# Loading the 32-blocks of a batch for the triangular substitution: four DMAs of 32 rows in place of one DMA with four copies as its outermost dimension

## The chip, the cores and the metric

The kernel runs on one core of one Trainium2 chip. The metric is the device time of one execution in microseconds (us), the median over several runs. The core has five engines that work side by side, each in the order of its own instruction queue: TensorE (PE, matmuls), VectorE (DVE), ScalarE (ACT), GpSimd (POOL) and SyncE (SP). SP only issues DMAs here; ACT and POOL issue some as well. The transfers themselves run on 16 DMA engines.

## The reference, cut to what matters

The reference is two network blocks over 512 tokens of width 1024. The part that the change touches is the bidirectional state recurrence of the second block, computed over 256 context tokens and then over the 512 latent tokens, in both directions:

```python
def wkv_step(S, inp):
    r, w, k, v, a, b = inp
    sa = jnp.einsum('dbhvk,dbhk->dbhv', S, a)
    S = S * w[..., None, :] + sa[..., None] * b[..., None, :] + v[..., None] * k[..., None, :]
    return S, jnp.einsum('dbhvk,dbhk->dbhv', S, r)

def wkv_bidir(S0, r, k_mod, v, decay, a_vec, b_vec):
    ...
    xs = tuple(to_scan(u) for u in (both(r), decay, k_mod, both(v), both(a_vec), b_vec))
    S, ys = lax.scan(wkv_step, S0, xs)
    ...
```

## The kernel before, in words

The recurrence is not run token by token. It is cut into chunks of 64 tokens, 12 chunks for each direction (4 of context, 8 latent). Two chunks make a batch, so there are 12 batches, taken in turn from the two directions. Within a chunk the recurrence becomes a matrix form that needs the inverse of a triangular 64x64 matrix for each of 8 heads. That inverse is found from the inverses of its two 32x32 diagonal blocks. A batch holds 2 chunks x 8 heads x 2 diagonal blocks = 32 such blocks.

Each batch passes through four steps, each a Python function:

- `ph_a` (L1130 on) loads what the chunk needs (`kb`, `kr`), scales it (`cs`, `ep`, `em`, `AR`, `BK`) and builds the products `AMB` with matmuls (`pA`, `ptb`).
- `ph_i` writes the 32 diagonal blocks from `AMB` to `atD` in DRAM by four DMAs of 32 KB (L1183), and loads them back as `LT` (L1186). In `LT` a partition holds one whole 32x32 block (1024 numbers, 4 KB), and the 32 blocks stand four times below each other, so that the 128 partitions hold four copies.
- `ph_s` runs the substitution on VectorE: 31 steps of two operations, a product into `Tm` from `LT` and `Ti` (L1198), and an addition into `Ti` (L1200). The four copies each work on another quarter of the columns, which `Ti` gets from a constant (L1193). Then four DMAs write `Ti` to `ttD` (L1203).
- `ph_b` loads the inverses into `TT` by four DMAs (L1217) and `v` into `XV` or `XW` (L1212, L1213), then works with matmuls (`pi`, `px`, `pW`, `pch`) and copies between PSUM and SBUF until the batch's state and output are there.

`LT` has two buffers, as `Ti` has; `Tm` has one. `batch(n)` calls `ph_a` and `ph_i` of batch n, then `ph_s` of the batch before, and `ph_b` of the batch two before.

The program is written step by step, but a planner settles the order in each engine's queue when the program is built. It walks through the instructions with estimates of their durations and waits, and it keeps an engine fed with whatever is ready: around the recurrence stand the projections of the second block (matmuls `pf`, `pt`, with weights loaded into `wr` at L298 and split by L305 on ACT and L306 on VectorE), the gates (`mth`, L1354) and the preparation of queries and keys (`dq`, `dk`, `gk`, `boD`). On the chip the order is then fixed; an instruction whose input is late holds up everything behind it on its queue.

All the loads named here go out from SP's queue, in order.

Of the kernel before, what the change touches and what calls it, by code (L numbers as in the profile page):

```python
# [191 lines left out]
def _build(ctx, tc, A, out, dbg, upto):  # L192
    nc = tc.nc
    V, SC, GP, PE, SY = nc.vector, nc.scalar, nc.gpsimd, nc.tensor, nc.sync
# [59 lines left out]
    def t2(name, dt=F32, w=512, tag="t2"):  # L254
        return cur["bp"].tile([128, w], dt, tag=tag, name=name, bufs=NB[tag])
# [7 lines left out]
    def ps(name, tag="mm"):  # L263
        return cur["pp"].tile([128, PB[tag][1]], F32, tag=tag, name=name, bufs=PB[tag][0])
# [21 lines left out]
    def vv(name):  # L286
        o, w = _VOFF[name]
        return vec[:, o:o + w]
# [182 lines left out]
    for i in range(4):  # L471
        t = t2("x%d" % i, w=1024, tag="t4")
# [569 lines left out]
    for f in range(8):  # L1042
        src, g = (ya[f], vv("norm_rec")[:, f:f + 1]) if f < 4 else (yb[f - 4], vv("norm_att")[:, f - 4:f - 3])
# [56 lines left out]
    atD = [dp.tile([2, 2, 8, 32, 32], F32, name="atD%d" % i) for i in range(4)]  # L1100
# [6 lines left out]
    def w1(name, shape=(4, 64), bufs=1, dt=F32):  # L1107
        p = rp if name == "AZ" else rpa if name in EARLY else rpb
        return p.tile([128] + list(shape), dt, tag=name, name=name, bufs=bufs)
# [10 lines left out]
    for d in range(2):  # L1120
        for e in range(2):
            t = rp.tile([128, 4, 64], F32, name="SI%d%d" % (d, e))
# [55 lines left out]
    def ph_i(d, AMB, bi):  # L1178

        for e in range(2):  # L1180
            for i in range(2):
                r0 = 64 * e + 32 * i
                SY.dma_start(atD[bi][e, i].rearrange("q s t -> s q t"),  # L1183
                             AMB[r0:r0 + 32, e, :, :, 32 * i:32 * i + 32].rearrange("p s f t -> p (s f) t"))
        LT = w1("LT", (32, 32), 2)
        SY.dma_start(LT.rearrange("p s t -> p (s t)"),  # L1186
                     atD[bi].rearrange("e i q s t -> (e i q) (s t)")[None].to_broadcast([4, 32, 1024]))
        return LT

    def ph_s(d, LT, bi):  # L1190
# [144 lines left out]
    def batch(n):  # L1335
        d, chs = batches[n]
        AMB = w1("AMB", (2, 2, 4, 192), 3)
        sts = {c - min(chs): ph_a(d, c, c - min(chs), AMB) for c in chs}
        LT = ph_i(d, AMB, n % 4)
        while loops:  # L1340
            ph_s(*loops.pop(0))
        loops.append((d, LT, n % 4))
        pend.append((n, (d, chs, sts, AMB, n % 4)))
        if len(pend) > 2:
            run_b()
# [61 lines left out]
    for j, nm in enumerate(("q", "k")):  # L1407
        g = qkg[:, 64 * j:64 * j + 64]
# [35 lines left out]
    for nm, c0, db in (("q", 512, "ql"), ("k", 1024, "kl")):  # L1444
        for hf in range(2):
# [30 lines left out]
            for f in range(2):  # L1476
                p = ps("dqT", "mm")
# [294 lines left out]
    def ot(name, bufs, w=512):  # L1772
        return orp.tile([128, w], F32, tag=name, name=name, bufs=bufs)
# [6 lines left out]
    for i in range(4):  # L1780
        t = op_.tile([128, 1024], F32, name="acc%d" % i)
# [13 lines left out]
    for c in range(4):  # L1795
        po2 = [ps("po2", "aux" if c % 2 else "mm") for _ in range(2)]
        for kh in range(2):
            hi, lo = split_chunk(load_chunk(A["w_out_2"], 256 * c, kt=4, nw=256, k0=4 * kh))
            for i in range(4):
                sl = slice(128 * i, 128 * (i + 1))  # L1800
                p = po2[i // 2][:, 256 * (i % 2):256 * (i % 2) + 256]
# [7 lines left out]
        for i in range(4):  # L1809
            t = ot("x2t", 3, 256)  # L1810
# [5 lines left out]
        for f in (2 * c, 2 * c + 1):  # L1816
            p = ps("xT", "aux")
            for i in range(4):
                PE.transpose(p[:, 128 * i:128 * (i + 1)], acc[i][:, 128 * f:128 * (f + 1)], ident)
            t = ot("xT", 2)  # L1820
# [217 lines left out]
    for i in (3, 2, 1, 0):  # L2038
# [5 lines left out]
        else:  # L2044
            t = t2("xn", w=1024, tag="t4")
# [33 lines left out]
    for p in range(16):  # L2079
        g, pr = p // 2, p % 2  # L2080
# [57 lines left out]
```

## Time and profile before

| what | value |
|---|---|
| median of 3 runs | 1914.18 us (1913.24 to 1919.19) |
| the profiled execution | 1915.38 us, of which the span from first to last instruction is 1913.6 us |
| TensorE | busy 1723.1 us, 90% of the span |
| VectorE | busy 1067.9 us, 56% |
| ScalarE | busy 616.6 us, 32% |
| GpSimd | busy 227.2 us, 12% |
| the batches of the recurrence | from about 495 us to about 1130 us of the span |
| the `LT` loads | 12, of 512 KB, the first issued at 502.7 us, the last at 1041.1 us |

The shares are means over the whole span, in which the projections come first, the recurrence with more projections next, and the experts at the end; each stage has another limit. A wait that the profile names ("<-DMA LT<-atD") is the event that came last before the waiting instruction started. The chain of work that ended last is followed back from the last instruction, at each step to what released it, so that its pieces add up to the span.

### The profile page before, as it was taken

How to read it: one execution, taken by the hardware profiler on the slowest of the kernel's cores; microseconds unless marked ns; L12 is line 12 of the kernel's file. 1: busy time of each engine (PE TensorE's matmuls, PEld its weight loads, DVE VectorE, ACT ScalarE, POOL GpSimd, SP SyncE). 2: the span in 40 equal slices, each digit the busy share in tenths (PEclk: the TensorE clock that was granted, in tenths of full speed). 3: DMA queues.
4: the chain of work that ended last, by engine and by line, in shares of the span. 5: the costliest groups of instructions: out<-in, count | busy, mean ns of one | idle time of the engine just before them, and what ended most of it. 6: DMA issues, size and time to landing. Idle time of an engine off the chain costs nothing.

```text
span 1913.6 us, 31328 instructions
## 1 busy us (share of the span) xinstructions
PE 1723.1 (90%) x12309; PEld 1225.2 (64%) x12310; DVE 1067.9 (56%) x2489; ACT 616.6 (32%) x1154; POOL 227.2 (12%) x254
## 2 busy tenths in 40 slices
PE   6999998976789798988989979979889999999998
PEld 3974678863456676877778756868854445444444
DVE  3545676565478655977877736866432323332332
ACT  4334464453443232333423424452311111111110
POOL 0200002011113001122110013300100000000000
PEclk8999999988898897989989988999989999999999
DMA  8336623558547545555664365717359999999997
GB/s 300 120 113 218 213 77 120 201 169 284 153 113 196 141 137 122 146 130 148 165 151 106 113 240 203 246 33 276 137 200 386 387 386 386 386 387 386 386 386 277
DMA packets 277023, 417.33 MB, mean 218 GB/s; under 512 B 105068, under 2 KB 128136, under 8 KB 276616
## 3 DMA queue, kind: packets, MB, share of 16 engines
q1 hardware_dynamic: 247976, 384.88, 60.5%
q10 hardware_dynamic: 25568, 16.78, 2.9%
q0 software_dynamic: 3328, 13.63, 2.5%
q8 instruction: 98, 1.61, 0.4%
q14 instruction: 53, 0.43, 0.1%
HBM read 371.70 MB, written 43.53 MB: 217 GB/s over the span
## 4 chain that ended last, share of the span: by engine, by line
PE 70%; DMA 11%; DVE 10%; ACT 3%; issue 3%; SPq 1%; POOL 1%; ACTq 0%; DVEq 0%; POOLq 0%
PE ped L1982 6%; PE peg L1943 6%; PE peu L1950 6%; PE pf L311 4%; PE pf L313 4%; PE pf L312 4%; PE pcb L2014 3%; PE po L1805 2%; DMA LT<-atD 2%; PE pt L313 2%; PE pt L311 2%; PE pW L1286 2%; PE pg L1916 2%; PE pt L312 2%; PE pg L1917 2%
## 5 line engine op out<-in xcount | busy, mean ns | idle before, releaser
L306 DVE TENSOR_TENSOR wl<-wr,wh 128x1024 fp32r<-128x1024 f32 x125 | 153.4, 1227 | 73.9 <-ACT wh L305 70.4
L305 ACT ACTIVATE wh<-wr 128x1024 fp32r<-128x1024 f32 x125 | 131.9, 1056 | 184.5 <-PE pf L312 91.9
L311 PE MATMUL pf<-h2h,wh 128*128 128x512 f32 x344 | 143.4, 417 | 20.0 <-ACT mth L1354 12.5
L313 PE MATMUL pf<-h2h,wl 128*128 128x512 f32 x344 | 141.4, 411 | 0.0
L312 PE MATMUL pf<-h2l,wh 128*128 128x512 f32 x344 | 141.3, 411 | 0.0
L1943 PE MATMUL peg<-wg,hTg 128*64 128x512 f32 x512 | 127.8, 597 | 0.0
L1982 PE MATMUL ped<-wd,hid 128*64 128x512 f32 (+1 forms) x528 | 125.5, 585 | 0.7 <-ACT hid L1966 0.7
L1950 PE MATMUL peu<-wu,hTg 128*64 128x512 f32 x512 | 126.0, 594 | 0.0
L1198 DVE TENSOR_TENSOR Tm<-LT,Ti 128x60 f32<-128x60 f32 (+24 forms) x372 | 86.6, 233 | 55.8 <-DMA LT<-atD 47.5
L2015 DVE TENSOR_TENSOR acc<-acc,pcb 128x512 f32<-128x512 f32 (+1 forms) x124 | 75.8, 665 | 39.9 <-PE pcb L2014 39.7
L1988 POOL TENSOR_TENSOR yl<-ey,yh 128x512 fp32r<-128x512 f32 x30 | 38.3, 1277 | 467.3 <-ACT yh L1987 467.3
L311 PEld LDWEIGHTS pf<-h2h,wh 128*128 128x128 f32 x344 | 67.1, 195 | 37.9 <-ACT mth L1354 12.8
L1200 DVE TENSOR_TENSOR Ti<-Ti,Tm 128x60 f32<-128x60 f32 (+24 forms) x372 | 83.8, 225 | 8.8
L1950 PEld LDWEIGHTS peu<-wu,hTg 128*64 128x64 f32 x512 | 44.4, 137 | 65.0 <-issue 63.3
L1982 PEld LDWEIGHTS ped<-wd,hid 128*64 128x64 f32 x528 | 38.9, 136 | 70.4 <-issue 64.7
L1943 PEld LDWEIGHTS peg<-wg,hTg 128*64 128x64 f32 x512 | 41.4, 137 | 61.9 <-issue 58.6
L313 PEld LDWEIGHTS pf<-h2h,wl 128*128 128x128 f32 x344 | 66.6, 194 | 21.7 <-issue 5.2
L312 PEld LDWEIGHTS pf<-h2l,wh 128*128 128x128 f32 x344 | 67.1, 195 | 17.4 <-issue 2.6
L1987 ACT ACTIVATE yh<-ey 128x512 fp32r<-128x512 f32 x30 | 18.9, 630 | 165.9 <-DVE ey L1986 94.1
L1923 DVE TENSOR_SCALAR hTg<-pg,gs,sh 128x128 f32<-128x128 f32 x64 | 25.3, 408 | 76.3 <-PE peu L1950 38.4
L1920 ACT ACTIVATE hTg<-pg,sh,gs 128x128 f32<-128x128 f32 x64 | 28.1, 456 | 122.6 <-PE peu L1950 55.4
L311 PE MATMUL pt<-wh,h1h 128*128 128x256 f32 x192 | 56.2, 295 | 5.8 <-ACT q L547 3.7
(958 smaller groups left out, 4327.8 us busy)
## 6 DMA issues: line engine op xcount, KB each, us to landing
wg<-in_w_exp_gate_dram SPq DMA_DIRECT2D x64, 1024.0 KB
wu<-in_w_exp_up_dram SPq DMA_DIRECT2D x64, 1024.0 KB
wd<-in_w_exp_down_dram SPq DMA_DIRECT2D x62, 1024.0 KB
wr<-in_w_in_dram SPq DMA_DIRECT2D x97, 512.0 KB
kb<-kbD SPq DMA_DIRECT2D x24, 384.0 KB
wr<-in_w_out_dram SPq DMA_DIRECT2D x16, 512.0 KB
LT<-atD SPq DMA_DIRECT2D x12, 512.0 KB
thD<-mth ACTq DMA_DIRECT2D x24, 256.0 KB
```

Source lines behind the costliest of these rows:

```text
L305: SC.activation(hi, raw, AF.Copy)
L306: V.tensor_tensor(lo, raw, hi.bitcast(F32), ALU.subtract)
L311: PE.matmul(p, ah, bh, start=start, stop=False)
L312: PE.matmul(p, ah, bl, start=False, stop=False)
L313: PE.matmul(p, al, bh, start=False, stop=stop)
L1198: V.tensor_tensor(tmp[:, :nj, :n], bc(LT[:, s, None, ts_], [128, nj, n]), bc(T[:, js, s:s + 1], [128, nj, n]), ALU.mult)
L1200: V.tensor_tensor(T[:, js, ts_], T[:, js, ts_], tmp[:, :nj, :n], ALU.add)
L1943: mm = PE.matmul(pg[64 * a:64 * a + 64, :], hT[:, k, 64 * a:64 * a + 64], gp[a][k // 4][:, k % 4, :], start=(k == 0), stop=(k == 7), tile_ ...
L1950: PE.matmul(pu[64 * a:64 * a + 64, :], hT[:, k, 64 * a:64 * a + 64], up[a][k // 4][:, k % 4, :], start=(k == 0), stop=(k == 7), tile_posit ...
L1982: PE.matmul(pd[64 * a:64 * a + 64, :], hid[:, m * k + 64 * a:m * k + 64 * a + 64], dn[q][a][:, k, 0:q1 - q0], start=(k == 0), stop=(k == 3 ...
L2014: PE.matmul(p, ohT[R, 128 * i:128 * (i + 1)], yy[R, qs], start=(z == 0), stop=(z == len(parts) - 1))
L2015: V.tensor_tensor(acc[i][:, qs], acc[i][:, qs], p, ALU.add)
```

## The change

`ph_i` loads `LT` by four DMAs, one for each group of 32 partitions, each of which reads the same 32 rows of 4 KB from `atD`. Before, it was one DMA whose source has a leading dimension of four copies with step 0. The bytes that move, their rows and where they land are the same; `atD`, the store before it and the substitution behind it are not touched.

```diff
         LT = w1("LT", (32, 32), 2)
-        SY.dma_start(LT.rearrange("p s t -> p (s t)"),
-                     atD[bi].rearrange("e i q s t -> (e i q) (s t)")[None].to_broadcast([4, 32, 1024]))
+        for g in range(4):
+            SY.dma_start(LT[32 * g:32 * g + 32].rearrange("p s t -> p (s t)"),
+                         atD[bi].rearrange("e i q s t -> (e i q) (s t)"))
         return LT
```

## Rows read from the trace of the kernel before

**Rows 1.** The page: busy time of TensorE, and the chain by engine.

```profile
PE 1723.1 (90%) x12309; PEld 1225.2 (64%) x12310; DVE 1067.9 (56%) x2489; ACT 616.6 (32%) x1154; POOL 227.2 (12%) x254
...
PE 70%; DMA 11%; DVE 10%; ACT 3%; issue 3%; SPq 1%; POOL 1%; ACTq 0%; DVEq 0%; POOLq 0%
```

**Rows 2.** Five of the chain's nine longest pieces in the recurrence: start, us, what.

```profile
502.68 10.43 DMA LT<-atD
550.55 11.31 DMA kb<-kbD
...
746.18 11.13 DMA TT<-ttD
...
917.76 9.58 DMA boD<-gk
955.36 13.02 DMA wr<-in_w_in_dram
```

**Rows 3.** The nine pieces as windows, sum (us, busy by engine); LT's four.

```profile
sum 103.32, PE 84.98 PEld 69.02 DVE 40.26 ACT 26.74 POOL 14.76; mean PE 9.44 PEld 7.67 DVE 4.47 ACT 2.97 POOL 1.64
...
sum 45.32, PE 39.09 PEld 31.98 DVE 13.56 ACT 13.70 POOL 6.21; mean PE 9.77 PEld 8.00 DVE 3.39 ACT 3.43 POOL 1.55
```

**Rows 4.** SP's queue, four of the 12 LT loads: start, us, line, what.

```profile
549.89 0.55 SPq L1186 DMA_DIRECT2D LT<-atD  x1
...
745.05 0.56 SPq L1186 DMA_DIRECT2D LT<-atD  x1
...
913.13 0.56 SPq L1186 DMA_DIRECT2D LT<-atD  x1
...
954.76 0.55 SPq L1186 DMA_DIRECT2D LT<-atD  x1
```

**Rows 5.** The chain's pieces of other DMAs: start, us, what.

```profile
689.91 1.63 DMA atD<-AMB
...
735.92 4.47 DMA kb<-kbD
...
986.68 1.87 DMA TT<-ttD
```

**Rows 6.** Who waited for LT (us, times), and VectorE's first use of two loads.

```profile
  DVE Tm L1198: 47.5, 8
...
513.13 0.19 DVE L1198 TENSOR_TENSOR Tm<-LT,Ti 128x31 f32<-128x31 f32 x1 [12.05 <-DMA LT<-atD]
...
1049.63 0.19 DVE L1198 TENSOR_TENSOR Tm<-LT,Ti 128x31 f32<-128x31 f32 x1 [4.75 <-DMA LT<-atD]
```

**Rows 7.** The load at 1041.07: SP's issue, DMA queue in 1042 to 1045, window.

```profile
1041.07 0.56 SPq L1186 DMA_DIRECT2D LT<-atD  x1
...
q1 hardware_dynamic: 51, 0.21, 21.0%
...
1042.00:1045.00 3.00, 3.00 (x57) 2.73 (x54) 2.70 (x11) 1.18 (x2) 0.00 (x0) 1.00 0.23 75
...
1600.00:1603.00 3.00, 3.00 (x14) 1.52 (x11) 0.17 (x1) 0.60 (x1) 0.00 (x0) 1.00 1.05 386
```

**Rows 8.** Windows by stage: us, engines' busy us (instructions), PEclk, DMA share, GB/s.

```profile
495.00:740.00 245.00, 205.57 (x1411) 154.11 (x1412) 162.54 (x405) 85.57 (x136) 37.33 (x49) 0.86 0.54 145
740.00:930.00 190.00, 168.50 (x1907) 145.48 (x1905) 146.86 (x477) 65.97 (x131) 35.78 (x49) 0.92 0.59 144
930.00:1130.00 200.00, 186.63 (x2092) 159.64 (x2093) 146.12 (x449) 67.61 (x127) 17.94 (x36) 0.95 0.51 141
```

**Rows 9.** Eleven gaps of TensorE behind the loads as windows: first, last, sum.

```profile
508.87:521.33 12.46, 0.00 (x1) 0.01 (x1) 8.09 (x16) 3.13 (x4) 1.42 (x3) 0.61 0.23 70
...
1049.63:1051.67 2.04, 0.00 (x1) 0.00 (x1) 1.94 (x8) 0.59 (x1) 0.00 (x0) 1.00 0.09 15
sum 58.45, PE 0.03 PEld 0.10 DVE 37.23 ACT 14.01 POOL 7.56; mean PE 0.00 PEld 0.01 DVE 3.38 ACT 1.27 POOL 0.69
```

**Rows 10.** SP's queue where four loads took long to issue.

```profile
873.61 10.73 SPq L1429 DMA_DIRECT2D gk<-kbD  x4
```

## The prediction, made before the changed kernel was run

> **What bounds the kernel now.** I read the page first. TensorE is busy for 90% of the span, and the chain of work that ended last gives it 70%, but 11% of the chain is DMA and another 10% VectorE [rows 1]. So the kernel is bound by TensorE on average and by something else in places; the question is whether the `LT` load is one of these places.
>
> Next I asked for the chain's longest pieces. Between 495 and 1130 us, the stage of the recurrence, its nine longest are all DMAs of 9.6 to 13.0 us [rows 2], and their sum is 103.3 us [rows 3]. Four are the `LT` load itself, 45.3 us together [rows 3]. SP's queue shows what the other five are: `kb` at 550.55, `TT` at 746.18, `wr` at 955.36 and `boD` at 917.76 [rows 2] went out 0.7, 1.1, 0.6 and 4.6 us after an `LT` load [rows 4], and so did one more `wr` behind another. On the chain an `atD` store costs 1.63 us, a `TT` load 1.87 and a `kb` load of 384 KB 4.47 when no `LT` load stands ahead [rows 5]. So `LT` costs time twice: VectorE waits for it, 47.5 us in 8 of the 12 batches [rows 6], and what is issued behind it lands late.
>
> Third, why it takes so long. The load at 1041.07 is the one with the least beside it. In 1042 to 1045 its queue moved 51 packets, 0.21 MB, in 21.0% of 16 engines' time, at 75 GB/s; the expert stage moves 386 GB/s [rows 7]. 21.0% of 16 x 3 us is 10.1 engine-us, or 198 ns for one 4 KB packet. The load has 128 such packets: 25.3 engine-us. VectorE got the data 8.56 us after the issue [rows 6, 7]. A load on four engines needs 6.3 us for its packets and leaves 2.2 us for issue, start and completion, which is near the whole of the 1.87 us of a small `TT` load [rows 5]; 16 engines would need 1.6 us. The busy share of about a quarter says the same: four engines work, twelve idle. Four is the size of the source's outermost dimension.
>
> **The change, part by part.** Removed: 12 DMAs of 512 KB. Added: 48 of 128 KB, each with 32 rows as the outermost dimension on both sides. The same 128 packets move. No row shows a 32-row DMA of 4 KB packets, so I bound it: below by the 32-row `atD` store, 1.63 us, above by the `kb` load of 128 rows, 4.47 us [rows 5].
>
> The Trainium skill, "DMA: Bandwidth & Descriptors", section "Rules for kernel authors", says that a leading zero-stride broadcast of c copies confines a DMA to at most c engines, and that a multiple of 16 belongs outermost; 21% of the engines' time in the trace agrees for four [rows 7]. By the Trainium skill, same page, section "Why a DMA increments its semaphore by 16 and not by 1", 32 outermost rows use 16 engines, which no row here shows for such rows.
>
> *The load.* Issuing one costs SP 0.55 us [rows 4]. So the fourth goes out 3 x 0.55 = 1.65 us after the first, and lands 1.6 to 4.5 us later: 3.3 to 6.1 us in all. I take 2.65 us for that landing, 4.3 in all: nearer to the store, which has the same 32 rows, than to the `kb` load, which moves three times the bytes of a part. The four `LT` pieces of the chain, 45.3 us [rows 3], become 17.2: **28.1 us less** (21 to 32 by the bounds).
>
> *What stands behind it.* The five other pieces sum to 103.3 - 45.3 = 58.0 us [rows 3]. Without the long queue I give `kb`, the two `wr` and `boD` 4.5 us each and `TT` 1.9 [rows 5], and each is issued 1.65 us later, because SP now has four DMAs ahead of it: 4 x 6.2 + 3.6 = 28.4, **29.6 us less**. By the chain alone 57.7 us would go.
>
> *What takes its place.* The chain follows one path only, and beside these waits TensorE was working: inside the nine pieces it is busy for 85.0 of 103.3 us, idle for 18.3 [rows 3]. Its queue is in a fixed order, so it gains only where it stood still. It stood still in the whole stage for 635 - 560.7 = 74.3 us [rows 8]. I matched its gaps to the loads: eleven, of 58.5 us together [rows 9], begin within 19 us of the issue of an `LT` load and end on ACT or VectorE work that was itself waiting behind `LT`, or behind a transfer held up by it. The first is plain: VectorE stood 12.05 us for `LT` [rows 6], and TensorE until 521.33 for an emptied PSUM tile [rows 9]. A load that lands earlier can take at most its 57.7 / 9 = 6.4 us from each gap; four gaps are longer than that and give 25.6, the seven shorter ones taken whole 22.9, together 48.5 us. The lower bound is the 18.3 us that TensorE idles inside the nine pieces themselves. I take the middle, **33 us**, because neither end fits: part of each gap lies after the landing, so 18.3 is too little, but VectorE was still busy for 37.2 of the gaps' 58.5 us [rows 9] with substitution steps and work queued behind them, of which some will be late for other reasons.
>
> *Costed at nothing.* SP's 36 more issues are 20 us of its queue over 540 us; they cost something only where SP itself is late, and the 1.65 us above is that price. `atD`, `Tm`, `Ti` and TensorE's own work don't change. TensorE's mean granted clock is 0.86 in 495 to 740 and 0.61 in the first gap [rows 8, 9], so it fell from its 2.4 GHz level to 1.2 there after standing still; fewer gaps may give some back, which I leave to the range.
>
> *The sum.* The profiled execution took 1915.4 us, 1.2 above the median of the runs. 1915.4 - 33 = 1882.4, or **1881 us** beside the median. Its own range is 48.5 to 18.3 us less, 1866 to 1896. The planner's order is a further unknown: it places 36 more instructions, and may order the other queues anew from 495 us on. A misplaced instruction costs about one gap of the kind seen here, up to 12.5 us [rows 9]; I widen both ends by that: 1854 to 1909.
>
> **The rivals.**
>
> *TensorE absorbs it.* TensorE is busy in 82% of the nine pieces [rows 3], and its order is fixed. If the work behind each load is late for another reason anyway (PSUM not emptied, a `wr` not split), only the idle time inside the pieces goes: 18.3 us, 1896 us. For it: 90% TensorE. Against: the gaps behind the pieces wait on engines that had themselves waited for `LT`.
>
> *Nothing changes.* The load stays on few engines, or the time lies in reading back what was just stored, not in the engines. Then 1912 to 1915 us. Against it: 51 packets in 3 us, evenly, is a rate limit and no latency [rows 7].
>
> *Slower: SP's queue becomes the limit.* Four `gk` loads took SP 10.73 us to issue at 873.61 [rows 10], while an `LT` load was under way. So issuing can be held up by what is already queued. If each of the four parts waits like that, at 10.73 / 4 = 2.7 us, the fourth goes out 8.1 us after the first, and `LT` lands at 10.7, no sooner than now. What stands behind goes out at 4 x 2.7 = 10.7 and lands 4.5 later, at 15.2 us, against 0.65 + 58.0 / 5 = 12.2 now: 3.0 x 5 = 15 us more, 1929 us. It decides from 2 us for each issue on, where both land as late as now (8.56 and 12.2). Against it: the `LT` issues themselves took 0.55 us each [rows 4], and the backlog at 873.61 may be the four engines' own, which the change takes away.
> The Trainium skill, "DMA: Bandwidth & Descriptors", section "Rules for kernel authors", also says that two transfers to disjoint partition halves serialize and should be one, which speaks for this rival; no run so far shows two parts of one load.
>
> **How the numbers follow.** Forecast 0.60; TensorE absorbs it 0.22; nothing changes 0.08; slower 0.10. The range 1854 to 1909 holds the first two, 0.82. Within 0.3% (5.7 us, about what a measurement of this kernel can tell from no change) is 1908 to 1920. Faster: the first two and a little of the third, 0.83. Same: 0.08. Slower: 0.09, since a little of the last case lies within 0.3%.
>
> **What the profile would show.** Right: 48 `LT` DMAs; issue to first use of about 4 to 5 us; VectorE's wait for `LT` from 47.5 to about 10 us; no DMA piece above 8 us on the chain between 495 and 1130; TensorE's idle time in the recurrence from 74 to about 41. Wrong: if `LT` lands in under 5 us and TensorE's idle time stays, the gaps had other causes; if L1186 or the instruction behind it shows long issues, the slow rival holds; if the queues' order differs far from the load, the planner's part is larger than the load's.

## The result, and the profile after

The changed kernel takes 1866.94 us (median of 4 runs, 1863.63 to 1868.35), the kernel before beside it 1914.12: a ratio of 0.975, with a 95% interval of 0.9728 to 0.9772. It is 47 us faster, where 33 were forecast; the time lies in the range. The profiled execution took 1868.35 us. Behind L1187 every line number is one higher than before.

The page of the changed kernel, to be read beside [rows 1]; its third line is a group (line, engine, operation, tiles, count | busy us, mean ns | idle time before it and what ended it):

```profile
PE 1715.4 (92%) x12309; PEld 1216.4 (65%) x12310; DVE 1068.7 (57%) x2489; ACT 617.4 (33%) x1154; POOL 230.4 (12%) x254
...
PE 73%; DVE 11%; DMA 7%; ACT 3%; issue 3%; SPq 2%; POOL 1%; ACTq 0%; DVEq 0%; POOLq 0%
...
L1199 DVE TENSOR_TENSOR Tm<-LT,Ti 128x60 f32<-128x60 f32 (+24 forms) x372 | 86.3, 232 | 14.0 <-DMA LT<-atD 5.3
```

DMA's share of the chain fell from 11% to 7%. VectorE's wait for `LT` fell from 47.5 us [rows 6] to 5.3.

The load of the fourth batch in the timeline, SP's queue and then VectorE's first use (start, us, engine, line, what, [idle before]):

```profile
679.93 1.71 SPq L1187 DMA_DIRECT2D LT<-atD  x4
...
684.64 0.19 DVE L1199 TENSOR_TENSOR Tm<-LT,Ti 128x31 f32<-128x31 f32 x1 [1.64 <-DMA LT<-atD]
```

Four issues take 1.71 us, and VectorE starts 4.71 us after the first. In the other three batches in which VectorE reached the load early it is 4.17 to 5.40 us, against 8.56 to 12.87 before where VectorE waited. In the second batch, and from the sixth on, the first use comes 10 us or more behind the issue with no wait at all: VectorE has other work until then.

The chain between 495 and 1130 us, to be read beside [rows 2] (start, us, what):

```profile
507.54 2.76 DMA LT<-atD
549.73 4.24 DMA kb<-kbD
560.45 6.72 DMA kbD<-nb
611.74 3.98 DMA LT<-atD
...
804.77 4.66 DMA wr<-in_w_in_dram
879.94 2.44 DMA boD<-gk
...
942.04 2.36 DMA TT<-ttD
```

The same kinds of transfer that took 9.6 to 13.0 us [rows 2] now take 2.4 to 4.7. The longest in the recurrence is a store from GpSimd's queue, 6.72 us.

The windows by stage (us, busy time by engine, granted clock, DMA share, GB/s), to be read beside [rows 8]. The stage ends earlier now, so it is cut at 1083, not at 1130:

```profile
495.00:740.00 245.00, 224.75 (x1630) 168.99 (x1628) 175.83 (x450) 92.82 (x151) 39.64 (x53) 0.91 0.59 156
740.00:930.00 190.00, 179.46 (x2098) 153.99 (x2097) 168.67 (x548) 73.75 (x146) 47.77 (x61) 0.97 0.62 165
930.00:1083.00 153.00, 149.38 (x1696) 127.47 (x1694) 112.00 (x338) 55.62 (x101) 7.60 (x21) 0.98 0.48 139
495.00:1083.00 588.00, 553.59 (x5420) 450.45 (x5417) 456.50 (x1333) 222.19 (x398) 95.01 (x135) 0.95 0.57 155
```

TensorE did the same work, 5420 matmuls in the whole stretch against 1411 + 1907 + 2092 = 5410 [rows 8]. Its idle time fell from 74.3 us to 588 - 553.6 = 34.4, so 39.9 us less. Its busy time fell from 560.7 to 553.6, 7.1 us less, at granted clocks of 0.91, 0.97 and 0.98 against 0.86, 0.92 and 0.95 [rows 8]. That the two make 47.0 us follows from where the stretch is cut; that the gain lies in this stage is shown by the first transfer behind it, the load of the outputs of the recurrence, which goes out at 1089.3 us now and went out at 1135.2 before.

How the gain divides into idle and busy time is not the same in every execution. From the first `LT` load to the load of the outputs (TensorE's busy time is the first after the length) it was, before, in the changed kernel and in a second execution of it (run 11 below):

```profile
502.68:1135.20 632.52, 556.37 (x5415) 456.50 (x5413) 453.28 (x1326) 217.92 (x392) 91.06 (x133) 0.91 0.54 142
...
506.25:1089.30 583.05, 547.05 (x5425) 448.25 (x5423) 453.83 (x1327) 218.25 (x393) 94.18 (x133) 0.95 0.57 154
...
499.89:1085.30 585.41, 542.88 (x5413) 445.34 (x5412) 452.17 (x1326) 217.48 (x389) 94.14 (x132) 0.95 0.56 153
```

Idle time is 76.2, 36.0 and 42.5 us: 40.2 less in the one execution and 33.7 in the other. Busy time is 9.3 and 13.5 us less.

### The profile page after: what moved, and what is told of

Read it like the earlier page. It is cut to its first block, busy times and chain, and to the rows that moved or that the text cites. A ratio compares the mean times of both kernels' runs of the same rounds, so it can differ in the third digit from the quotient of the medians.

```text
span 1866.5 us, 31358 instructions
## 1 busy us (share of the span) xinstructions
PE 1715.4 (92%) x12309; PEld 1216.4 (65%) x12310; DVE 1068.7 (57%) x2489; ACT 617.4 (33%) x1154; POOL 230.4 (12%) x254
## 4 chain that ended last, share of the span: by engine, by line
PE 73%; DVE 11%; DMA 7%; ACT 3%; issue 3%; SPq 2%; POOL 1%; ACTq 0%; DVEq 0%; POOLq 0%
PE ped L1983 7%; PE peg L1944 6%; PE peu L1951 6%; PE pf L311 5%; PE pf L313 4%; PE pf L312 4%; PE pcb L2015 3%; PE po L1806 2%; PE pt L311 2%; PE pt L313 2%; PE pt L312 2%; PE pg L1917 2%; PE pg L1918 2%; DVE Tm L1199 1%; DMA kb<-kbD 1%
## 5 line engine op out<-in xcount | busy, mean ns | idle before, releaser
L1983 PEld LDWEIGHTS ped<-wd,hid 128*64 128x64 f32 x528 | 39.4, 136 | 71.4 <-issue 67.7
L1924 DVE TENSOR_SCALAR hTg<-pg,gs,sh 128x128 f32<-128x128 f32 x64 | 25.3, 409 | 75.3 <-PE peu L1951 38.4
```

Source lines behind the costliest of these rows:

```text
L1983: PE.matmul(pd[64 * a:64 * a + 64, :], hid[:, m * k + 64 * a:m * k + 64 * a + 64], dn[q][a][:, k, 0:q1 - q0], start=(k == 0), stop=(k == 3 ...
```

## The experiments

In the traces of before and after TensorE's matmuls start in the same order up to about 770 us, but for two short swaps, and in a widely different one behind it. So all kernels here but the repeat of the changed one hold every engine's queue in a given order, by constraints on the order of issue alone; it is the order of the changed kernel where nothing else is said. "Held" below stands for that. The runs are spread over several chips, each with runs of the kernel before beside them, so between chips it is the ratios to these that are compared. The profile follows the chain of some of these kernels back to a part of the span only (run 2's to 1019 us, run 3's to 597), so chains are quoted for the others.

**1. Four DMAs in the order of before** (the edit: the change, with every queue held as before it).

> The four DMAs of the changed kernel, with every engine's queue held in the order of the kernel before, instruction by instruction; the same results are computed. Theory A, the load's landing is what changed the time and the planner's new order is worth little: LT is used 4 to 5.5 us after its first issue, VectorE's wait for it is under 12 us, and the time is 1866 to 1876. Theory B, a good part of the 47 us came with the new order: the landing is the same, but the time is 1881 to 1895, near the 33 us that were predicted for a fixed order.

1860.81 us, ratio 0.9714 (0.9668 to 0.976). The whole gain is there without the new order; the time lies 5 us under the range that was named for theory A, and far from theory B's.

**2. One DMA in the order of after** (the edit: the load of before, with every queue held as after).

> The one DMA of the kernel before, with every queue held in the order of the changed kernel; the same results are computed. Theory A: LT is used 8.5 to 12 us after its issue and the time is back at 1905 to 1920. Theory B: the order alone keeps part of the gain, 1885 to 1900.

1917.19 us, ratio 1.0027 (1.0001 to 1.0052), `LT` first used 10.3 to 11.1 us after its issue where VectorE waited, 34.1 us in all. The new order alone gains nothing.

**3. Four DMAs that stay on few engines.** The blocks lie in DRAM with q outermost (the four stores into `atD` are changed to fit), so that each part has 4 as its outermost dimension at the source, and 32 rows at the destination:

```diff
-            SY.dma_start(LT[32 * g:32 * g + 32]..., atD[bi].rearrange("e i q s t -> (e i q) (s t)"))
+            SY.dma_start(LT[32 * g:32 * g + 32]..., atD[bi].rearrange("q e i s t -> (e i) q (s t)"))
```

> Four DMAs in the order of the changed kernel, but the blocks lie in atD with the head index first, so that the source of each DMA has an outermost dimension of four; the bytes, the rows of 4 KB and the results are the same. Theory A, the number of engines sets the landing, and it is the outermost dimension: four DMAs on four engines need 6.3 us for their packets as one does, LT is used 8.5 to 12 us after the first issue, time 1905 to 1920. Rival, the load got shorter since four DMAs start and run side by side: landing 4 to 5.5 us, time 1864 to 1872.

1898.01 us, ratio 0.9935 (0.9909 to 0.9961). The fourth batch again:

```profile
688.61 2.66 SPq L1189 DMA_DIRECT2D LT<-atD  x4
...
698.90 0.19 DVE L1202 TENSOR_TENSOR Tm<-LT,Ti 128x31 f32<-128x31 f32 x1 [7.16 <-DMA LT<-atD]
```

10.29 us to the first use, 8.47 to 11.87 in the others: nearly as late as before. So cutting the load in four brings little on landing; the outermost dimension does. The time, though, is some 14 us shorter than before, outside the range of theory A, and 19 us shorter than run 2, which has the same order and is the one to compare with. VectorE's wait is 28.6 us, against 34.1 there.

The traces show a part of the reason. A DMA reports its landing by raising a semaphore, a counter, and the trace has the time of each step. By them the whole tile is there 9.6 us after the first issue in the mean of the twelve batches (8.3 to 11.7), in run 2 after 11.1 (9.0 to 12.9), and what SP issues in the 5 us behind the load lands 6.9 us after its own issue in the mean, in run 2 after 10.6. So this backlog is shorter. In the three batches in which no 4 KB packets but the load's are on the way, one takes 185 to 210 ns, in run 2 249 to 333. Why they are faster is not shown: the parts and the layout in DRAM were changed together.

**4. Two DMAs of 64 rows, two copies each.**

```diff
-        for g in range(4):
-            SY.dma_start(LT[32 * g:32 * g + 32]..., rows)
+        for g in range(2):
+            SY.dma_start(LT[64 * g:64 * g + 64]..., rows[None].to_broadcast([2, 32, 1024]))
```

> The load is made by two DMAs of 64 rows, each of two copies (outermost dimension 2), with every queue in the order of the changed kernel. Theory A (the outermost dimension decides over how many engines a DMA goes, and the time follows from how long those engines are held): both DMAs share two engines, the tile lands at about twice the 8.6 to 12.3 us of before, so 17 to 25 us after its first issue, VectorE waits for it for 80 us or more, what stands behind it is held up twice as long, and the kernel is slower than before by about as much as the change made it faster: 1945 to 1985 us. Rival B (it is the number of DMAs that counts, more and smaller ones being in flight together): two DMAs lie between one and four, 1885 to 1914 us.

1967.86 us, ratio 1.0297 (1.0263 to 1.0331): slower than before by more than the change gained. The fourth batch, and then some of its chain:

```profile
703.40 1.11 SPq L1189 DMA_DIRECT2D LT<-atD  x2
...
720.36 0.19 DVE L1202 TENSOR_TENSOR Tm<-LT,Ti 128x31 f32<-128x31 f32 x1 [13.85 <-DMA LT<-atD]
```

```profile
554.75 14.45 DMA kb<-kbD
...
624.20 17.02 DMA LT<-atD
...
853.32 16.15 DMA wr<-in_w_in_dram
```

16.96 us to the first use, 14.4 to 17.8 where VectorE waited, and 12.6 to 16.2 us for what stands behind. The landing comes somewhat earlier than the 17 to 25 us that were expected, and VectorE's wait was overestimated: 46.9 us, not 80, because it waits for the load in five batches only. The number of DMAs went from one to two and the time rose, so theory B falls.

**5. Eight DMAs of 16 rows.**

> The load is made by eight DMAs of 16 rows, the other instructions in the order of the changed kernel. Theory A (four parts already go over all engines; more parts only add issues): SP spends some 3.4 us a batch on issues in place of 1.7 us, LT is first used 5 to 7 us after the first issue, and the kernel takes 1867 to 1882 us. Rival (smaller parts land sooner, so what is left of the waits shrinks too): 1850 to 1863 us.

1876.40 us, ratio 0.9809 (0.9779 to 0.9839).

```profile
678.49 4.08 SPq L1189 DMA_DIRECT2D LT<-atD  x8
...
685.72 0.19 DVE L1202 TENSOR_TENSOR Tm<-LT,Ti 128x31 f32<-128x31 f32 x1 [3.04 <-DMA LT<-atD]
```

7.23 us to the first use in place of 4.71, a little over the 5 to 7 that were expected, and eight issues take 4.08 us in place of 1.71. Four more issues put the load off by what they take on SP, and bring nothing; the rival falls.

**6. A backlog behind an early load.** Behind the four, a fifth DMA in the form of before, into a scratch buffer in DRAM that nothing reads:

```diff
             SY.dma_start(LT[32 * g:32 * g + 32]..., rows)
+        SY.dma_start(LX[:, :, 0:1024], rows[None].to_broadcast([4, 32, 1024]))
```

> The changed kernel in its own order, and behind the four DMAs of each batch a fifth that nobody reads: the load of before, four copies outermost, 512 KB, into a scratch tensor in DRAM. LT lands as early as in the changed kernel, but what stands behind it on SP's queue meets the four long queues of before. If VectorE's wait alone counts: 1866 to 1872. If the transfers behind count for about half of the gain, as the terms of the prediction have it (29.6 of 57.7): 1885 to 1897.

1905.29 us, ratio 0.995 (0.9929 to 0.9972). `LT` is used early (4.0 to 5.9 us), VectorE waits 8.3 us for it, and yet 38 of 47 us are gone, more than was expected of the backlog. The chain of the profiled execution, which took 1896.56 us and was the fastest of the ten:

```profile
503.33 9.13 DMA kb<-kbD
549.74 8.06 DMA kb<-kbD
...
733.96 8.05 DMA LX<-atD
742.03 3.84 DMA cst<-in_cst_dram
...
815.14 9.91 DMA wr<-in_w_in_dram
943.75 8.81 DMA wr<-in_w_in_dram
```

What SP issues in the 5 us behind the load lands 8.4 us after its own issue in the mean, against 4.2 in the changed kernel and 11.0 before. The third and fourth lines show a second way in which the load costs time. Nobody reads `LX`, but SP itself stands still until it has landed: `cst` goes out 0.02 us after that. In the trace `cst` waits for the semaphore that `LX` raises, and raises it next. It was so in the kernel before, where SP waited 5.6 us at this place, until the `LT` load of 745.05 [rows 4] had landed:

```profile
757.06 0.33 SPq L275 DMA_DIRECT2D cst<-in_cst_dram  x1
```

In the changed kernel SP waits for no `LT` load. The price of the backlog contains these waits.

**7. The same bytes without the backlog** (four more DMAs of 32 rows into the scratch buffer, in place of the fifth).

> The changed kernel in its own order with, behind the four DMAs of each batch, four more of the same form that copy the same 512 KB into a scratch buffer in DRAM that nothing reads: the bytes of the load are moved twice, as in the run with the unread four-copy DMA, but on all engines. Theory A (there it was the four engines that were held up which cost 38 us): the second four cost 1.7 us of issues on SP and about 1.5 us of all engines in each of 12 batches, partly on the path: 1868 to 1885 us, LT first used 4 to 6 us after its issue. Rival (it was the second 512 KB, or the time on SP's queue): about 1905 us again.

1883.44 us, ratio 0.9844 (0.9808 to 0.988). That lies in the range of theory A. So of the 38 us, up to 18 are the price of moving 512 KB more and of issuing it (four issues here, one there); the four engines' backlog is worth the difference of the ratios, 0.0106 or 20 us (with an interval of about 8 either way), up to 38.

**8. The load from GpSimd's queue** (one DMA with four copies, `GP.dma_start` for `SY.dma_start`).

> The load is one DMA with four copies, as before, but it is issued by GpSimd, so that what stands behind it on SP's queue doesn't queue behind its packets, only shares the four engines with them; SP doesn't wait for the DMAs into atD either. All other instructions stand in the order of the changed kernel. Theory A1 (most of the gain comes from the transfers behind the load on the same queue): LT still lands 9 to 13 us after its issue and VectorE waits for it 30 to 50 us in all, but most of the gain is kept: 1870 to 1892 us. Rival A2 (most of the gain is VectorE's own wait): 1900 to 1920 us, with TensorE's gaps behind VectorE's waits as before. If the four engines serve both queues in turn and the transfers behind the load suffer the same, it is 1900 us or more too, but then with pieces of kb, TT or wr over 8 us in the chain.

1896.34 us, ratio 0.9908 (0.988 to 0.9937), VectorE's wait 39.4 us. In its chain:

```profile
738.09 10.89 DMA TT<-ttD
...
862.85 12.76 DMA gk<-kbD
```

The load went out on GpSimd's queue at 735.53 and 861.30 us, and the two transfers shown, each one of a group of four, on SP's 2.6 and 1.6 us behind it. They are held up although the load is on another queue. The time lies between the ranges of A1 and of the other two cases; by the pieces of the chain it is the third: it is the engines that are held, not only the queue, and so this run doesn't part the two prices.

**9. The load late, with nothing held up** (GpSimd doubles the tile and halves it in place).

```diff
             SY.dma_start(LT[32 * g:32 * g + 32]..., rows)
+        GP.tensor_tensor(LT, LT, LT, ALU.add)
+        GP.tensor_scalar(LT, LT, 0.5, None, op0=ALU.mult)
```

> The changed kernel in its own order; behind the four DMAs GpSimd doubles the tile and halves it again in place, so that VectorE gets it some 4 to 5 us later in each of 12 batches while nothing on SP's queue and none of the DMA engines is held up. It prices VectorE's own wait alone, as the run with the unread four-copy DMA priced the transfers behind the load alone (38 us of 47). Theory A1 (the two parts add up): VectorE's wait for the tile goes from 5 us to 30 to 50 us, but the time rises by 8 to 20 us only, to 1875 to 1887 us. Rival A2 (the chain is shared: either of the two delays alone brings most of the time back, so their prices add up to more than the whole): 1895 to 1910 us.

1900.08 us, ratio 0.9941 (0.9919 to 0.9963), 36 us above the changed kernel on the same chip. The two instructions in the first batch, and who waited for the tile (us, times):

```profile
507.56 1.89 POOL L1192 TENSOR_TENSOR LT<-LT 128x1024 f32<-128x1024 f32 x1 [3.92 <-DMA LT<-atD]
509.55 2.78 POOL L1192 TENSOR_SCALAR LT<-LT 128x1024 f32<-128x1024 f32 x1
512.36 0.19 DVE L1204 TENSOR_TENSOR Tm<-LT,Ti 128x31 f32<-128x31 f32 x1 [11.34 <-POOL LT L1192]
...
  DVE Tm L1204: 21.3, 3
```

As a number this was rival A2, though VectorE's wait for the tile, 21.3 us in three batches, stayed under the 30 to 50 that were expected. But GpSimd's own queue stood behind these instructions too, and VectorE's products took longer beside them, so a control was needed.

**10. The control to that** (the same two instructions, written to the tile's other buffer, so that VectorE takes the load as it lands).

> The control to the late tile: GpSimd makes the same two instructions of the same shapes behind the four DMAs, but writes into the other buffer of LT, which nothing reads, so that VectorE takes the tile as it lands. (The load so has one buffer, not two; each load of the changed kernel is issued after the substitution before it has ended, so this should hold nothing up.) If the late tile itself made the 36 us by which that run was above the changed kernel, this one takes 1864 to 1876 us. If it was GpSimd (what stands behind the two instructions on its queue, VectorE slowed beside them), it takes 1890 us or more. In between, the difference of the two runs is the price of VectorE's own wait.

1877.03 us, ratio 0.9801 (0.9773 to 0.9829), VectorE's wait 9.7 us. So at most 13 us (9 by the ratios) of the 36 were GpSimd's, and the late tile's own price is at least about the difference of the ratios, 0.0140 or 27 us (about 7 either way). At least, because the control slows VectorE more than run 9 does: it is busy for 1095.2 us here, for 1085.5 in run 9 and for 1068.7 in the changed kernel.

**11. The changed kernel and run 1 once more, on one chip.**

> The changed kernel once more, to stand on the same chip as the four DMAs in the order of before: 1864 to 1870 us.

> Four DMAs with every queue in the order of before, once more, beside the changed kernel on the same chip. If the new order costs something, this takes 1857 to 1863 us and is 4 to 9 us shorter than the changed kernel; if the 6 us between the two earlier runs were scatter, the two agree within 2 us.

1863.80 us (0.9752; 0.9728 to 0.9777) and 1860.69 us (0.9731; 0.9706 to 0.9756). The order of before is 3 us better by the medians, between the two cases that were named and less than the 0.3% that can be told, and the intervals overlap. So a second gain is not shown.

## Why the prediction was right, point by point, and where it was too small

**The load goes from 4 engines to 16.** Shown. In the traces the landing of a four-copy load raises its semaphore in four steps, that of each part of run 3 in four, of run 4 in two, and that of each part of 32 rows in sixteen; where there are fewer than sixteen, one more step stands about 1 us behind the issue. Of the load's 4 KB packets four are on the way at a time before and in run 3, two in run 4, and about sixteen in the changed kernel. The working of the prediction, 25.3 us of packets over the number of engines and 2.2 us around them, can be laid beside three counts of engines:

| engines | packets + 2.2 us | measured, issue to first use where VectorE waited |
|---|---|---|
| 16 (four DMAs) | 1.6 + 2.2, and 1.65 for the issues: 5.4 | 4.2 to 5.4 |
| 4 (before) | 6.3 + 2.2 = 8.5 | 8.6 to 12.9 |
| 4 (run 3) | 8.5, and 1.9 for the issues: 10.4 | 8.5 to 11.9 |
| 2 (run 4) | 12.7 + 2.2 = 14.9 | 14.4 to 17.8 |

The landing of 4.3 us that was forecast lies in what was measured. The 25.3 us go by 198 ns for a packet, read from the load with the least beside it; in the fifth and eighth batch before, a packet took 286 and 281 ns, by which the same sum gives 11.4 and 11.2 us, and 12.0 and 11.9 were measured. With sixteen engines the sum is too long, since an issue takes 0.42 us and not 0.55. The Trainium skill, "DMA: Bandwidth & Descriptors", section "Rules for kernel authors", names the copies as the limit, and the rows for four and two copies agree with it. Run 3 shows that four outermost at the source keep a part on four engines even where the destination has 32 rows.

**`LT` and what stands behind it cost time twice.** Shown: each alone brings back a time clear of noise, 27 us for VectorE's own wait (runs 9 and 10; up to 36) and 20 us for the backlog (runs 6 and 7; up to 38). That the lower two just make the 47 us may be luck: each has an interval of 7 to 8 us, and the backlog of run 6 is milder than that of before (8.4 us to landing against 11.0). The prediction's two chain terms, 28.1 and 29.6, were about equal; the measured prices agree with that, but are too wide to show it. Without the controls the two would have come to 36 + 38 = 74 us, and run 6 alone would have been read as "mostly the backlog". The prediction did not see the waits of SP itself for the load (run 6), which the measured price of the backlog contains; they were not priced apart.

**The gaps of TensorE.** This term was sized too small: "I take the middle, 33 us", between 18.3 and 48.5. The idle time fell by some 40 us in the one execution and by 34 in the other, so by 1 to 7 us more than forecast. The middle was held back because VectorE was busy in most of the gaps with work that might be late for other reasons. What in each gap is left over was not measured one by one.

**TensorE's clock**, left to the range and so put at nothing in the sum, is the other term. The busy time fell by 7 to 9 us in the one execution, by where the stretch is cut, and by 13.5 in the other. A matmul of 128x512 takes 409 ns before and 408 after at the upper level of the clock, and 683 and 712 at the lower; of the stage's matmuls 507 started at the lower level before, 303 and 269 in the two executions after. So the 14 us between forecast and result are 1 to 7 us of the gaps and 7 to 13 of the busy time, which goes with the clock: leaving the clock out of the sum weighs at least as much as the size of the gaps.

**The planner's order**, for which 12.5 us were added at both ends, is worth 3 us on one chip (run 11) and 5 to 7 by the ratios of runs 2 and 1, although it differs widely from about 770 us on.

**SP's issues.** 36 more of them, 0.42 us each now, cost what they were counted as, a delay of the load itself: with eight parts the first use moves by 2.5 us and the time by 13 (0.9809 against 0.9752 is 11).

**The rivals.** That TensorE absorbs it fell: its idle time went. That nothing changes fell: the load lands in 4 to 6 us, and runs 3 and 4 make the number of engines the cause. That SP's queue becomes the limit fell: the issues didn't grow to 2 us, and the longest issue of a `gk` load went from 4.68 us to 1.56. The rule of the Trainium skill, "DMA: Bandwidth & Descriptors", section "Rules for kernel authors", that two transfers to disjoint partition halves serialize and should be one, points the other way here, where the one transfer has its copies outermost: what it saves in issues is less than what the copies cost, and four parts beat one.

**The signs that were announced** all came: 48 DMAs, a first use 4 to 5 us after the issue, a wait of 5 us where about 10 were named, no DMA piece above 8 us in the recurrence (the one of 8.41 us at 1091.5 is the load of its outputs, behind it), and 34 us of idle TensorE where 41 were named.

## What to carry to other kernels

Look at how many DMA engines a load can use before its size: a load whose source has its copies outermost runs on as many engines as there are copies (shown here for two and four), and can be cut into one DMA for each copy. Its price is its own landing and everything that is issued behind it on the same engines, even from another queue, so look for other transfers on the chain that follow it by a microsecond, and for DMAs that the issuing engine holds back until the load has landed. When such a cost is priced by adding a delay, run a control that adds the same work without the delay; here the controls took a quarter off the one price and half off the other. And profile the same kernel twice before a gain is split into idle and busy time.

## What the runs showed of the hardware that was not expected

- A backlog on four engines holds up transfers of another engine's queue as well: with the load on GpSimd's queue, `TT` and `gk` from SP's took 10.9 and 12.8 us of the chain (run 8, where it stood as the third case).
- The issue of a part with 32 plain rows took SP 0.42 us, of the load with copies 0.56 (`LT` before) and of the part with a three-dimensional source 0.63 (run 3), all as medians.
- VectorE's product of 128x31 numbers, 0.19 us otherwise, took 1.77 us in the control where it began 0.17 us after GpSimd's 128x1024 addition of 1.89 us: the two end together. It was so in several batches of run 10:

```profile
900.23 1.89 POOL L1193 TENSOR_TENSOR LT<-LT 128x1024 f32<-128x1024 f32 x1 [1.51 <-DVE Tm L1205]
900.40 1.77 DVE L1205 TENSOR_TENSOR Tm<-LT,Ti 128x31 f32<-128x31 f32 x1
```

- The four parts on few engines (run 3) land nearly as late as the one load, but the kernel is 14 us faster than before. Their 4 KB packets take 185 to 210 ns against 249 to 333; why is left open.
